# A sum-of-reciprocals kernel: one written-out list of operations replaced by another

## The chip, the cores and the metric

The kernel runs on one core of a Trainium2 chip. Its time is the device time of one execution in microseconds, measured with the profiler off; the median of three such runs of the kernel before is 168.22 us (168.21 to 168.27). A separate profiled execution gives the trace; all durations and moments below come from it, and moments are counted from the start of its span. Engines are written as the profile does: PE is the matrix engine, DVE the vector engine, ACT the scalar (activation) engine, POOL the GpSimd engine and SP the engine that issues the transfers.

## The reference: what is computed

```python
# x: float32, 32 x 512 x 1024, all positive
def reference(x):
    return np.sum(1.0 / x, axis=-1).astype(np.float32)
```

The input has 16384 vectors of 1024 numbers, 67.1 MB; each vector gives one number. Nothing is reused, so every byte is loaded once and used once.

The kernel doesn't divide. It takes the two halves a and b of a vector (512 numbers each) and uses 1/a + 1/b = (a + b) / (a b). The reciprocal of the product a b is made as exp(-ln(a b)) on ACT, with a scale S = 2^17 inside the logarithm that is multiplied out again at the end. One logarithm and one exponential serve two numbers in this way.

## The kernel before: rows, ring, banks and a list of operations

The 16384 vectors lie as 128 partitions by 128 "rows": row r is one vector on each partition, 512 KB in all. The last two rows are each loaded and worked on as two half rows, so that the numbering goes from row 0 to row 129: 0 to 125 are whole, 126 to 129 are halves of 256 KB. Rows live in three places:

- `ring`, 40 row slots in SBUF; row r takes slot r mod 40, so the transfer of row r can't be issued until everything that reads row r - 40 out of the ring is done;
- `prod`, 22 slots in SBUF for products, in which ACT also works;
- `ps`, 8 banks of PSUM.

The order of all work is a list of words, `PLAN`, written out in full and read by a loop at the end of the function. A word is a letter, a row, a count (`+2`) and a bank or product slot (`@6`):

| word | engine, line | what it does |
|---|---|---|
| `Dn` | SP, L187 | load the next n rows (split where the ring wraps round) |
| `Pr+n` | POOL, L199 | product a b of n rows, into `prod` |
| `Cr@b` | PE, L209 | copy the second half of row r to bank b (multiply by the identity) |
| `Vr` | DVE, L220 | product of row r from the ring and the copy in PSUM |
| `Wr` | DVE, L220 | product of row r, both halves from SBUF |
| `Lr+n@p` | ACT, L242 | logarithm of n products, in place, slots p on |
| `Er+n` or `Er+n@b` | ACT, L251 | exponential: in place, or into banks b on |
| `Sr@b` | PE, L232 | a + b of row r into bank b (two multiplications by the identity, accumulated) |
| `Rr` | DVE, L267 | multiply and sum up: the row's result |

A row's product is made in one of three ways (P, V or W). Its last step has two forms. Where the list has an S, R takes the 512 sums in PSUM times the 512 reciprocals in `prod`. Where the E went to PSUM, R takes the whole row of 1024 from the ring times the reciprocals in PSUM, each used twice; the first form costs PE time, the second DVE time.

Each engine does its own words in the order of the list. Between engines, an operation waits for what it reads, and for the last reader or writer of the ring slot, product slot or bank that it overwrites; `note` records this from the order of the list. SP is in order too: a transfer that waits for a ring slot holds back all transfers behind it. When rows 0 to 113 have their results, six small transfers write these out (L289); a last one (L291) writes the rest after the last R.

The lines that issue the loads and those that make the two forms of R are

```python
                    m = min(n, R - a, LAST - r) if r < LAST else 1
                    inst = nc.sync.dma_start(
                        out=ring[:, a : a + m, at : at + 2 * w],
...
                if r in halves:
                    row = prod[:, p, :w]
                else:
                    row = ring[:, q % R, at : at + 2 * w]
```

Of the kernel before, what the change touches and what calls it, by code (L numbers as in the profile page):

```python
# [11 lines left out]
def kernel(  # L12
# [23 lines left out]


    PLAN = """
        D2 D10 D14 D14 P0+2 C3@3 S2@0 V3 P2 L0+2@0 C11@3 S3@1 E0+2@6 P4+2 V11 L2+2@2 R0 S6@2
        E2+2 R1 P6+2 L4+2@4 R2 R3 E4+2@6 S7@0 P8+2 L6+2@8 R4 S10@1 E6+2 R5 P10 L8+2@10 R6 R7  # L40
        S11@2 E8+2@6 L10+2@6 R8 E10+2 R9 D11 R10 R11 P12+2 C19@3 S14@0 V19 P14+2 L12+2@12
        S15@1 E12+2@6 S18@2 R12 P16+2 L14+2@16 R13 E14+2 R14 P18 L16+2@18 R15 S19@0 E16+2@6
        P20+2 L18+2@14 R16 S22@1 E18+2 R17 D9 P22+2 L20+2@20 R18 R19 E20+2@6 S23@2 P24+2
        L22+2@0 R20 E22+2 R21 L24+2@2 R22 R23 E24+2@6 P26 C27@3 R24 S26@0 P28+2 V27 R25 D7
        L26+2@4 C35@3 E26+2 S27@1 P30+2 V35 L28+2@8 R26 S30@2 R27 E28+2@6 P32+2 L30+2@10 R28
        S31@0 E30+2 R29 P34 L32+2@12 S34@1 R30 R31 E32+2@6 P36+2 S35@0 L34+2@6 R32 E34+2 R33
        D7 P38+2 S38@2 L36+2@16 R34 R35 E36+2@6 S39@1 P40+2 L38+2@18 R36 C43@3 E38+2 R37 D6
        S42@0 P42 L40+2@14 V43 R38 E40+2@6 P44+2 R39 S43@2 L42+2@20 R40 E42+2 S46@1 R41 D3
        P46+2 L44+2@0 R42 R43 E44+2@6 S47@0 P48+2 L46+2@2 R44 S50@2 E46+2 R45 P50 L48+2@4
        R46 C51@3 R47 E48+2@6 S51@1 P52+2 V51 R48 D6 L50+2@8 C59@3 E50+2 R49 P54+2 S54@0  # L50
        L52+2@10 V59 R50 E52+2@6 R51 S55@2 P56+2 L54+2@12 R52 E54+2 S58@1 R53 D5 P58
        L56+2@16 R54 R55 E56+2@6 S59@0 P60+2 L58+2@6 R56 S62@2 E58+2 R57 D4 P62+2 L60+2@14
        R58 R59 E60+2@6 S63@1 P64+2 L62+2@18 R60 S66@0 E62+2 R61 D4 P66 L64+2@20 R62 C67@3
        R63 E64+2@6 P68+2 S67@2 V67 R64 L66+2@0 S70@1 R65 D4 E66+2 P70+2 L68+2@2 R66 R67
        S71@0 E68+2@6 P72+2 L70+2@4 R68 D3 E70+2 R69 D2 C75@3 P74 L72+2@10 S74@2 R70 V75
        P76+2 E72+2@6 R71 S75@1 L74+2@8 R72 D2 E74+2 R73 D2 P80 S78@0 L76+2@12 R74 P81
        L80@16 R75 S79@2 E76+2@6 P78+2 L81@17 R76 D2 S81@1 E80@5 E81 R80 L78+2@6 W82 E78+2
        R81 R77 D1 D1 D1 D1 D1 P88 C85@6 S85@1 R78 P83 L88@18 V85 E88@7 R79 P84 S84@0
        L82+2@14 R88 E82+2@5 P86+2 L84+2@19 R82 D1 E84+2 R83 D1 D1 D1 C90@7 P91 L86+2@0
        S91@2 R85 P93 V90 E86+2@5 R84 P92 S90@1 L90+2@2 R87 L93@21 W89 L92@10 R86 D1 D1 D1  # L60
        D1 E93@7 P94 S97@0 E92@6 R93 E90+2 P97 S94@3 L89@11 R92 E89@7 P95 L97@8 R91 S95@4
        E97 R90 L94+2@4 W96 R97 P101 C99@6 L96@9 R89 E94+2 S100@0 P98 V99 E96@5 L101@12 R95
        P100 S99@1 L98@13 R96 E101@7 L99+2@16 R101 E98@6 P104 C103@5 R94 E99+2 S105@2 R98
        P102 L104@18 V103 E104@7 W105 L102+2@6 R100 P107+2 C106@6 L105@14 R104 E102+2@4
        S108@0 V106 E105 R102 L106+3@19 P109 S107@3 R103 P110 E106+3 R105 S106@4 R99 P111+2
        L109+2@0 R107 S112@1 R108 E109+2@6 R106 L111+2@10 P114 R109 S111@0 E111+2 R110 P113
        L114@15 R111 C115@7 P116 L113@2 R112 E114@6 V115 E113@5 S117@0 P117 R114 L116@3
        L115@8 P118 E116@7 R113 S118@1 E115@6 P119 L117+2@12 R116 E117+2 R115 P120 S120@2
        L119@9 R117 P121 L120@4 S121@3 R118 E119@7 E120 R119 P122 L121@5 S122@0 E121 R120
        P123 L122@18 R121 E122 W124 L123@6 R122 L124@7 W125 S125@1 E123@7 E124@6 R123 P126  # L70
        L125@14 P127 L126@16 S127@0 R124 E125 P128 L127@17 S128@2 E126@7 P129 R125 E127
        S129@3 L128@19 R126 L129@20 E128 R127 E129 R128 R129
    """.split()

    Ln = mybir.ActivationFunctionType.Ln
# [246 lines left out]
```

## Time and profile before

| | |
|---|---|
| median of three runs | 168.22 us |
| profiled execution: span from first to last instruction | 166.3 us |
| what lies around the span, by the median | 1.9 us |
| busy: PE, ACT, DVE, POOL | 132.5, 132.3, 128.3, 128.2 us |
| loaded | 67.11 MB, 404 GB/s over the span |
| first product (POOL), second (POOL) | 5.66 us, 17.75 us |
| last DVE instruction ends | 164.0 us |

The page gives no other total for the profiled execution than its span; the 1.9 us around it is the median less the span, and sums below are made against the span and carried over with it. The four engines have nearly the same busy time, some 80% of the span, and the transfer engines are busy almost from end to end. For such a kernel the busy shares say little: what counts is which of five nearly equal streams of work is late at which place, so the profile is read by its chain of waits and by the moments at which rows land.

### The profile page before, as it was taken

Reading aid. Unit: us, or ns where it says so; the run is one execution under the profiler, and the core shown is the slowest. Engines: PE = TensorE matmul, PEld = TensorE weight load, DVE = VectorE, ACT = ScalarE, POOL = GpSimd, SP = SyncE. Lnnn points to the kernel's source line nnn. Section 1 sums busy time; section 2 is a strip of 40 time slices with the busy share of each in tenths; the row PEclk is TensorE's granted clock in tenths of the full one; section 3 lists DMA queues with packets and bytes.
Section 4 is the critical chain, followed back from the end, with each engine's and each line's share of the span. In section 5 each row is a group of like instructions: output and inputs, shape, how many; then the busy total and the mean of one; then the engine's idle time right before and its main releaser. Section 6 shows DMA issues by size and latency. Waiting matters only on the chain.

```text
span 166.3 us, 1348 instructions
## 1 busy us (share of the span) xinstructions
PE 132.5 (80%) x292; PEld 55.2 (33%) x292; DVE 128.3 (77%) x282; ACT 132.3 (80%) x157; POOL 128.2 (77%) x81
## 2 busy tenths in 40 slices
PE   0000799978855999999999999988699979989982
PEld 0000333333312444444343433324234424433351
DVE  0000119885787699898998898989899999999994
ACT  3040073949995899999799999996999999999992
POOL 1500795069995999999999999948977869999860
PEclk9999999999996999999999999999999999999999
DMA  5999999999998989999999999999999999999940
GB/s 189 536 394 394 441 441 441 441 441 441 441 441 349 509 368 446 430 417 438 441 434 434 406 426 446 429 424 424 414 437 437 414 410 428 410 409 410 400 139 4
DMA packets 5768, 67.26 MB, mean 404 GB/s; under 512 B 1536, under 2 KB 1536, under 8 KB 3200
## 3 DMA queue, kind: packets, MB, share of 16 engines
q1 hardware_dynamic: 5760, 67.18, 95.6%
q8 instruction: 2, 0.03, 0.1%
q14 instruction: 6, 0.05, 0.1%
HBM read 67.11 MB, written 0.07 MB: 404 GB/s over the span
## 4 chain that ended last, share of the span: by engine, by line
DMA 57%; PE 18%; ACT 8%; DVE 6%; POOL 6%; issue 3%; SPq 1%; ACTq 0%; POOLq 0%; DVEq 0%
DMA ring<-in_x_dram 57%; PE ps L232 15%; POOL prod L199 6%; ACT prod L242 4%; PE ps L209 3%; ACT ps L251 2%; DVE ring L267 2%; DVE prod L267 2%; ACT prod L251 2%; DVE prod L220 1%; SPq L187 1%; DVE sums L267 0%; ACTq L242 0%; POOLq L199 0%; DVEq L317 0%
## 5 line engine op out<-in xcount | busy, mean ns | idle before, releaser
L199 POOL TENSOR_TENSOR prod<-ring 128x1024 f32<-128x1024 f32 (+2 forms) x75 | 127.5, 1727 | 33.5 <-DMA ring<-in_x_dram 27.1
L232 PE MATMUL ps<-ring,ident 128*128 128x512 f32 (+1 forms) x260 | 116.9, 596 | 5.2 <-DVE sums L267 4.5
L242 ACT ACTIVATE prod<-prod 128x1024 f32<-128x1024 f32 (+2 forms) x78 | 68.5, 892 | 24.9 <-DVE prod L220 14.3
L267 DVE CUSTOM_DVE_ANT_1 ring<-ring,ps 128x1024 f32<-128x1024 f32 (+1 forms) x65 | 76.4, 1208 | 8.9 <-ACT ps L251 8.7
L232 PEld LDWEIGHTS ps<-ring,ident 128*128 128x128 f32 x260 | 49.2, 193 | 71.7 <-issue 51.6
L267 DVE CUSTOM_DVE_ANT_0 prod<-prod,ps 128x512 f32<-128x512 f32 (+1 forms) x63 | 40.9, 677 | 0.4 <-PE ps L232 0.4
L209 PE MATMUL ps<-ring,ident 128*128 128x512 f32 x32 | 19.3, 689 | 25.7 <-DMA ring<-in_x_dram 24.0
L251 ACT ACTIVATE ps<-prod 128x1024 f32<-128x1024 f32 (+2 forms) x41 | 34.1, 838 | 4.5 <-DVE sums L267 3.7
L251 ACT ACTIVATE prod<-prod 128x1024 f32<-128x1024 f32 (+3 forms) x37 | 34.4, 931 | 0.9
L220 DVE TENSOR_TENSOR prod<-ring,ps 128x512 f32<-128x512 f32 x16 | 10.9, 684 | 26.3 <-PE ps L209 26.3
L209 PEld LDWEIGHTS ps<-ring,ident 128*128 128x128 f32 x32 | 6.0, 213 | 36.0 <-issue 21.4
L267 DVE DVE_READ_ACCUMULATOR2_ANT sums<- 128x1 f32 x130 | 10.7, 82 | 0.0
L220 DVE TENSOR_TENSOR prod<-ring 128x512 f32<-128x512 f32 x6 | 4.1, 688 | 0.1
L84 ACT ACT_TABLE_LOAD x1 | 1.3, 1283 | 0.7 <-PEq L306 0.7
L267 DVE CUSTOM_DVE_ANT_0 prod<-prod,ps,sums 128x256 f32<-128x256 f32 x2 | 0.9, 475 | 0.0
masks.py:197 POOL MEMSET ident<- 128x128 f32 x1 | 0.2, 204 | 0.3 <-POOLq L306 0.3
masks.py:199 POOL TENSOR_SCALAR_AFFINE_SELECT ident<-ident 128x128 f32<-128x128 f32 x1 | 0.3, 292 | 0.1
L306 POOL MEMSET const-float32-0.0<- 128x1 f32 x1 | 0.1, 98 | 0.2 <-issue 0.2
L306 POOL MEMSET const-bfloat16-1.0<- 128x1 bf16 x1 | 0.1, 101 | 0.0
L306 POOL MEMSET const-uint8-127<- 128x1 uint8 x1 | 0.1, 101 | 0.0
L306 POOL MEMSET const-float32-1.0<- 128x1 f32 x1 | 0.1, 98 | 0.0
## 6 DMA issues: line engine op xcount, KB each, us to landing
ring<-in_x_dram SPq DMA_DIRECT2D x2, 7168.0 KB, 41.2
ring<-in_x_dram SPq DMA_DIRECT2D x2, 3584.0 KB, 29.3
ring<-in_x_dram SPq DMA_DIRECT2D x2, 3072.0 KB, 31.9
ring<-in_x_dram SPq DMA_DIRECT2D x3, 2048.0 KB, 34.0
ring<-in_x_dram SPq DMA_DIRECT2D x1, 5632.0 KB, 30.3
ring<-in_x_dram SPq DMA_DIRECT2D x5, 1024.0 KB, 31.8
ring<-in_x_dram SPq DMA_DIRECT2D x1, 5120.0 KB, 16.5
ring<-in_x_dram SPq DMA_DIRECT2D x1, 4608.0 KB, 30.7
```

The costliest lines, as they stand in the source:

```text
L84: nc.scalar.add_instruction(mybir.InstLoadActFuncSet(name=nc.get_next_instruction_name(), act_func_set_id=act_sets.index("natural_log_exp_ ...
L187: inst = nc.sync.dma_start(out=ring[:, a : a + m, at : at + 2 * w], in_=x_v[:, q : q + m, at : at + 2 * w],)
L199: inst = nc.gpsimd.tensor_tensor(out=prod[:, p : p + m, :w], in0=ring[:, a : a + m, at : at + w], in1=ring[:, a : a + m, at + w : at + 2 * w],
L209: inst = nc.tensor.matmul(ps[:, b, : place(r)[2]], lhsT=ident, rhs=xs(r, 1), start=True, stop=True,)
L220: inst = nc.vector.tensor_tensor(out=prod[:, p, :w], in0=xs(r, 0), in1=in1, op=mult)
L232: inst = nc.tensor.matmul(ps[:, b, : place(r)[2]], lhsT=ident, rhs=xs(r, h), start=h == 0, stop=h == 1,)
L242: inst = nc.scalar.activation(out=pg, in_=pg, func=Ln, scale=S)
L251: inst = nc.scalar.activation(out=rc, in_=pg, func=Exp, scale=-1.0)
L267: inst = nc.vector.tensor_tensor_reduce(out=row, in0=row, in1=other, scale=S, scalar=total if q in summed else 0.0, op0=mult, op1=add, acc ...
L306: nc = _bacc.Bacc("TRN2", target_bir_lowering=False, num_devices=1)
```

## The change

Only the text of `PLAN` differs; the loop, the buffers and the lines after it are the same, six lines further down (L232 is L238, L242 is L248 and so on). Counted by words:

| | before | after |
|---|---|---|
| transfers of rows | 33 | 32 |
| first transfers, rows | 2, 10, 14, 14, 11, 9, 7, 7 | 15, 14, 11, 8, 10, 8, 8, 6 |
| P of one row, of two | 38, 33 | 72, 14 |
| C and V (product through PSUM) | 16 | 23 |
| W (product from SBUF) | 6 | 3 |
| L of one row, of two, of three | 23, 50, 1 | 66, 27, 2 |
| E of one row, of two, of three | 23, 50, 1 | 112, 7, 0 |
| S of whole rows | 62 | 60 |
| R over a whole row of 1024 | 64 | 66 |
| R over 512 sums | 62 | 60 |

The half rows 126 to 129 are left out of the lower eight lines; each has 4 P, 4 L, 4 E, 3 S and 4 R of half size in both lists. The ring's wrap splits the words D19 and D11 of the new list into 11 and 8 and into 6 and 5 rows.

Before, an `L` of two rows is mostly followed at once by the `E` of the same two rows, in row order. After, rows are taken out of order within about ten rows, and between the `L` and the `E` of a row there are mostly other words. The diff, cut to the beginning, the parts that are spoken of below, and the end:

```diff
     PLAN = """
-        D2 D10 D14 D14 P0+2 C3@3 S2@0 V3 P2 L0+2@0 C11@3 S3@1 E0+2@6 P4+2 V11 L2+2@2 R0 S6@2
-        E2+2 R1 P6+2 L4+2@4 R2 R3 E4+2@6 S7@0 P8+2 L6+2@8 R4 S10@1 E6+2 R5 P10 L8+2@10 R6 R7
...
-        P123 L122@18 R121 E122 W124 L123@6 R122 L124@7 W125 S125@1 E123@7 E124@6 R123 P126
-        L125@14 P127 L126@16 S127@0 R124 E125 P128 L127@17 S128@2 E126@7 P129 R125 E127
-        S129@3 L128@19 R126 L129@20 E128 R127 E129 R128 R129
+        D15 P2 P0 C1@0 C4@1 V1 P3 L0+3@0 V4 L3+2@3 E4@2 R4 E3 E2@3 C7@4 R2 P11 E1@5
+        P10 P13 D14 S3@6 L10+2@5 E11@7 P5+2 C8@0 V8 P9 R1 L5+2@9 S0@1 L8@11 V7 E6
+        L7@13 E7@2 P14 E5@3 R11 L13+2@7 S6@0 S8@5 E0 R3 R7 E14 C12@4 S14@7 P18 V12 R5
+        D19 L12@15 C28@6 P17 P15 C16@2 E13@4 P21 L18@14 E8 R0 R14 R13 S19@3 V28 V16
...
+        R21 R32 S24@3 E38 E29@7 E35 R31 L39@12 S35@0 E37@4 R34 R22 C44@1 D8 P40 P41
+        R35 R38 L42+2@6 L46+2@14 E39@2 P56 E42+2 P57 R37 V44 S47@6 S43@0 L40@20 R39
+        S42@5 P53 P54 P51 C48@4 E47 E46@1 R43 R29 E33@2 L44+2@3 R24 E36@0 L41@18 R46
+        P52 R36 E41@7 R47 E45@3 P50 C55@1 R42 R41 L56@13 V48 E40 L48@21 P49 E44@0 R33
+        E56@6 S51@5 P58+2 S55@7 V55 E48@4 S40@2 P62+2 L53+2@0 R44 R48 L57@19 D8 E54@1
...
+        E114+2 R113 P122 E116@4 R111 L117@8 R115 L118@6 R114 E117 L119@9 E118@1 R116
+        L120@12 P123 E119 S122@3 S123@2 E120@5 L121@17 E121 R117 R118 L122@11 R119
+        P126 R120 P127 E122 R121 P128 P129 W124 L123@10 R122 W125 L124@13 E123 E124@4
+        S125@0 R123 L125@14 L126@0 E125 E126@1 R124 R125 L127@7 L128@4 E127 S127@7
+        R126 S128@5 S129@6 L129@3 R127 E128 E129 R128 R129
     """.split()
```

## The prediction

> **What bounds the kernel now.** I read the page first (busy shares, the 40 slices), then the end of the chain of waits, then the timelines of the opening and of the last 8 us, then the groups with shapes kept apart.
>
> ```profile
> PE 132.5 (80%) x292; PEld 55.2 (33%) x292; DVE 128.3 (77%) x282; ACT 132.3 (80%) x157; POOL 128.2 (77%) x81
> ...
> DMA  5999999999998989999999999999999999999940
> ...
> HBM read 67.11 MB, written 0.07 MB: 404 GB/s over the span
> ```
>
> No engine is full; the transfer engines are, from slice 2 to slice 38. The end of the chain shows how the stream and the end hang together:
>
> ```profile
> 147.18 10.17 DMA ring<-in_x_dram
> 157.34 0.02 issue
> ...
> 158.81 1.72 PE ps L232 x4
> ...
> 163.54 0.08 DVE sums L267
> 163.63 0.39 DVE prod L267
> ```
>
> The chain rides on the transfers until row 124 lands. The trace's landing records (one per transfer engine) have row 125 complete at 158.7, and in the timeline PE begins then and stops no more:
>
> ```profile
> 158.81 4.54 PE L232 MATMUL ps<-ring,ident 128*128 128x512 f32 x16 [1.12 <-DVE sums L267]
> ...
> 163.54 0.47 DVE L267 CUSTOM_DVE_ANT_0 prod<-prod,ps,sums 128x256 f32<-128x256 f32 x1
> ```
>
> Those 16 matmuls are S125, S127, S128 and S129: the fixed tail. Row 125 lands, 0.1, 4.54 on PE to 163.35, then R129 to 164.0; 5.3 us in all. (The wait is put down to DVE; the landing falls in the same 0.1 us.) So the bound is the stream of transfers up to row 125 plus 5.3 us. The median is 168.22, the span 166.3; the 1.9 between them is carried over.
>
> The opening shows when work can start:
>
> ```profile
> 5.66 2.34 POOL L199 TENSOR_TENSOR prod<-ring 128x1024 f32<-128x1024 f32 x1 [4.36 <-DMA ring<-in_x_dram]
> ...
> 17.75 8.20 POOL L199 TENSOR_TENSOR prod<-ring 128x512 f32<-128x512 f32 x4 [9.75 <-DMA ring<-in_x_dram]
> ...
> 17.81 2.04 PE L209 MATMUL ps<-ring,ident 128*128 128x512 f32 x2 [17.81 <-DMA ring<-in_x_dram]
> ```
>
> Each engine starts when a whole transfer has landed: two rows at 5.66, ten more at 17.75, 1.21 us per row.
>
> **The change, part by part.**
>
> *The stream.* The same 67.1 MB. The last 21 pieces (4, 4, 4, 3, 2, 2, 2, 2 rows, nine single rows, four halves) are alike in both lists, and in all there are 32 pieces for 33. A row costs 1.21 us in pieces of 14 (17.75 to 34.69) and 1.28 us as a single row (landings of 117 to 125: 148.5 to 158.7), so 0.07 us per piece: -0.1 us. Each piece must be issued before the queue runs dry. From issue (0.74) to landing (5.66) D2 took 4.9 us, of which 2.5 are its two rows, so the lead has to be 2.4 us.
>
> *The opening.* The first piece has 15 rows and lands at 17.75 + 3 x 1.21 = 21.4. What goes is the early start of POOL and ACT on two rows (2.34, and 1.06 + 1.03) and 3.7 us of everything else: between 0 (hidden) and 3.7 + 2.1 = 5.8 us on ACT. I take 0 for the time, because work left over is done while the stream, which doesn't wait for it, goes on until 158.7; the cover is the free time worked out below, and if it is gone the cost is one to one. PE's slow start (first matmuls 0.85 to 0.9 us, later 0.43) comes 3.6 us later too and is paid inside the 4.0 us that PE waits for rows 15 to 28.
>
> *Work per engine.* Steps from start to start, from rows in which an engine ran without a wait: POOL 2.34 for two rows, 1.25 for one; DVE 1.14 (whole row), 0.61 (sums), 0.60 (product); PE 0.43 a matmul; ACT 0.96 for two rows, 0.52 for one, and 0.13 more when an E follows at once on its own L (1.09 between such starts, 0.96 otherwise).
>
> ```profile
> 88.01 1.05 ACT L242 ACTIVATE prod<-prod 128x1024 f32<-128x1024 f32 x1
> 89.09 1.06 ACT L251 ACTIVATE prod<-prod 128x1024 f32<-128x1024 f32 x1
> 90.05 1.04 ACT L242 ACTIVATE prod<-prod 128x1024 f32<-128x1024 f32 x1
> ```
>
> - ACT: 66 more instructions. 100 two-row and 46 one-row become 34 and 178 (and two triples of 1.4 for two): 63.4 less, 68.6 more, +5.3. But E right behind its own L falls from 52 cases to 18: -4.4. Sum 132.0 to 132.8.
> - POOL: 19 doubles fewer (-44.5), 34 singles more (+42.5): 127.5 to 125.6.
> - DVE: 2 more whole-row R (+2.3), 2 fewer of the other (-1.2), 7 V more and 3 W fewer (+2.4): 125.8 to 129.3.
> - PE: 7 C more (14 matmuls, +6.0), 2 S fewer (8, -3.4): 123.1 to 125.7.
>
> The sums of before agree with its busy times to 2% except PE's, whose records overlap and include slow starts.
>
> The Trainium skill, ScalarE: Activation LUTs, section What ACT_TABLE_LOAD costs, speaks against splitting: every ACTIVATE has 186 ns of fixed cost, of which back-to-back ones overlap 93. By that rule 66 more would be an estimated +6.1 us on ACT and a list near 138 us, which would end ACT past the stream. The trace agrees on the step (0.52 against 0.48 per row) but shows what the rule doesn't have: the overlap is lost when E reads what the L before it wrote.
>
> *Does it fit in?* I ran the sums forward in list order: P, C, S and W not before their row lands (the landings of before by rows loaded), L not before its product, R not before its E and S. For before this gives DVE's end 164.1 (the trace: 164.0). For after: L0+3 needs V1, P2 and P0 (two POOL steps: 23.9), and from there to the same last E at 163.3 ACT has 139.4 us for 132.8 of work, 6.6 free. It must wait for late rows at L5 (1.2), L18 (1.6), L58 (0.6), L61 (1.1) and some small ones, 5 in all, the last big one at 92. About 1.6 us of slack remain from there to the end; POOL keeps 0.7 behind P86; DVE and PE over 2.5. The end comes out at 163.7 by DVE (R123 is now 0.61 in place of 1.14), but S129 still ends at 163.35, and R129 needs 0.05 + 0.47 + 0.08 after it: 163.9, so -0.1.
>
> *Waits on banks and slots.* Compared pair by pair in those sums, a producer comes later than its consumer wants it at six places in after (S6 on V8 1.6, S8 on R1 1.0, C44 on R31 0.5, S47 on R22 1.4, S51 on R42 0.5, L48 on V48 1.6) and at seven in before (up to 2.5). All six lie before 78 us. Behind S6 on PE stand C12 and C28, but C28 waits 4.0 for its row; behind S47 stands C48, which waits 4.0; behind L48 stand all later L and E, and L58 and L61 then wait 1.6 less. I take 0 in sum; between 0 and 1.6.
>
> *SP.* D19's second half needs R5 (37.2 by the sums, queue dry at 52), D10 needs S9 (48.6; 62), D8 R22 (66.7; 75), the second D8 R33 (79.5; 84.4), all later ones have 11 us or more. The tightest lead is 4.9 us against the 2.4 needed: 2.5 us of room. Before, by the same sums, leads were 20 us or more. D5 waits for the late S85 (131, needed at 157).
>
> Sum: -0.1 (tail and pieces overlap there) = 163.9 for DVE's end, 168.1 us.
>
> **The rivals.**
>
> *ACT or POOL end behind the stream (slower).* For it: from L61 on ACT has no free time, and in before ACT fell behind its own forward sum by 1.06 us within 55 us (L78+2 at 110.69 against 109.6). At that rate 65 us cost 1.25, inside the 1.6; at twice the rate 2.5, so +0.9; with the 1.6 of L48 unhidden on top +2.5. POOL's 0.7 is thinner still. Against it: the list leaves its E and R more time behind their producers than before (E behind P is over 2 us in 40 cases, 3 before). It decides once 1.6 us are lost on ACT after 92: 169.0 to 170.6.
>
> *The stream runs dry at the second D8 (slower).* If R33 is more than 2.5 us late against 79.5, each further us goes straight to the end; L48's 1.6 us wait is near it. Against: R33's E stands before L48. With 2 us over: 170.1.
>
> *The stream gets faster (faster).* Of the 16 transfer engines the first is done with D2 0.4 us before the last, with row 125 2.0 us: the last ones are held up singly, at moments that coincide with small transfers on the two instruction queues (2 and 6 packets on the page). Another list shifts these. Between +0.8 and -1.6 us; half of the gain, -0.8: 167.4.
>
> *The change does nothing for the time because the opening is hidden* is the forecast; its opposite, the opening in full, would be 168.2 + 5.8 = 174, and no cover speaks for it.
>
> **How the numbers follow.** 0.2% of 168.2 is 0.34 us, about what a measurement can tell. The stream and fixed tail as now: 0.57, 168.1, with 0.35 inside 0.34 us and the rest split by the instruction queues, 0.10 faster and 0.12 slower. ACT or POOL late: 0.25, slower. Stream dry: 0.08, slower. Stream faster: 0.10. Faster 0.20, same 0.35, slower 0.45. The range takes the half gain below and ACT's rival above: 167.4 to 170.4; the likeliest case alone is 167.6 to 168.7.
>
> **What would show it.** Right: first product at 21.4, POOL's wait for P18 ending near 38.3, row 125 landing at 158 to 159.5, PE without a gap from there, ACT's sum of busy time near 133 to 140 (records overlap). Wrong: row 125 landed and S125 waiting over 0.5 us for a bank; L123 waiting for nothing with rows long landed; slices of DMA share under 8 near 84 us; row 125 outside 158 to 159.5.

## The result and the profile after

The changed kernel takes 169.08 us (median of five executions, 168.71 to 170.1), the kernel before 168.27 beside it (168.21 to 168.4): a ratio of 1.0055, with a 95% interval of 1.003 to 1.008. It is 0.8 us slower. The forecast was 168.1 us, no change. Ratios are of fast executions alone: of the old list with the big opening, further down, four of twelve executions took 171.1 to 171.7 us and count as slow.

The page of the changed kernel. Its profiled execution is one of the quicker ones, 168.89 us with a span of 167.1.

```profile
PE 132.3 (79%) x298; PEld 56.3 (34%) x298; DVE 131.5 (79%) x286; ACT 134.7 (81%) x223; POOL 126.2 (76%) x96
...
PEclk9999999999999999996999999999999999999999
DMA  7999999999799999999999999999999999999940
```

The busy times of POOL and DVE moved as the sums had them: -2.0 and +3.2 for -1.9 and +3.5. ACT's rose by 2.4 where the sum had 0.8; its records overlap, so that its busy time is not the sum of its steps. (PE's can't be compared: its records lengthen with the granted clock, the row PEclk.) The transfer engines are as full as before. Nothing on this page says where 0.8 us went.

The timeline of the opening: the first product starts at 21.8, not at 21.4.

```profile
21.81 9.75 POOL L205 TENSOR_TENSOR prod<-ring 128x512 f32<-128x512 f32 x7 [20.50 <-DMA ring<-in_x_dram]
```

The chain of waits, in order of time (start, us, what):

```profile
79.27 1.13 DVE ring L273
80.40 0.02 DVE sums L273
...
80.44 0.33 SPq L193
...
80.81 21.14 DMA ring<-in_x_dram
...
110.45 29.75 DMA ring<-in_x_dram
...
140.27 2.47 POOL prod L205 x2
...
153.21 1.30 POOL prod L205
...
154.53 0.03 ACT prod L248
...
163.53 0.32 ACT prod L257
...
163.87 0.15 DVE prod L273
...
164.35 0.39 DVE prod L273
```

The DVE result at 80.40 is R33, and what SP issues at 80.44 is the second D8 (rows 66 to 73), with the next piece right behind it. (The chain of before has a result on DVE ahead of an issue too, at 101.9 us.)

The end differs as well. Before, the chain goes with the transfers up to row 124, as shown above. Here it leaves them at 140.2 and goes over POOL, which works from P109 on almost without a gap, and from 154.53 over ACT, which has waited for P120 and has no gap from L120 to E129. R128 waits for E128 (over at 163.83), and R129 follows R128. PE is through with S129 at 163.91. In the kernel before it was DVE that had no gap from W125, at 158.69, to the end; PE was through at 163.35, and R129 began at 163.54, right behind R128. Two windows of before show it:

```profile
core 0: us, PE busy (x) PEld busy (x) DVE busy (x) ACT busy (x) POOL busy (x), PEclk, DMA share, GB/s
160.00:162.00 2.00, 2.00 (x9) 1.43 (x8) 2.00 (x5) 2.00 (x7) 2.00 (x4) 1.00 0.20 36
162.00:164.00 2.00, 1.35 (x7) 0.85 (x5) 2.00 (x10) 1.30 (x5) 0.23 (x1) 1.00 0.02 4
```

The trace has 16 landing records for each transfer, one per transfer engine. From them:

| | before | after |
|---|---|---|
| first piece complete | 5.59 (2 rows) | 21.74 (15 rows) |
| row 125, mean of the 16 engines | 157.18 | 157.92 |
| row 125, complete (last engine) | 158.67 | 159.20 |
| last DVE instruction ends | 164.03 | 164.76 |
| from row 125 to that end ("tail") | 5.36 | 5.56 |

So 0.5 us come with the stream and 0.2 behind it. The theories to be told apart were: the second D8 is issued too late (the rival with a chance of 0.08); the bigger opening; and ACT or POOL being behind the stream (the rival with 0.25).

### The profile page after: what moved, and what is told of

Read it like the earlier page. It is cut to its first block, busy times and chain, and to the rows that moved or that the text cites. A ratio compares the mean times of both kernels' runs of the same rounds, so it can differ in the third digit from the quotient of the medians.

```text
span 167.1 us, 1420 instructions
## 1 busy us (share of the span) xinstructions
PE 132.3 (79%) x298; PEld 56.3 (34%) x298; DVE 131.5 (79%) x286; ACT 134.7 (81%) x223; POOL 126.2 (76%) x96
## 4 chain that ended last, share of the span: by engine, by line
DMA 53%; POOL 20%; DVE 11%; ACT 6%; issue 3%; PE 3%; another core or an unknown queue 1%; SPq 1%; DVEq 0%
DMA ring<-in_x_dram 53%; POOL prod L205 20%; DVE ring L273 6%; ACT prod L248 3%; DVE prod L273 3%; ACT prod L257 2%; PE ps L238 2%; ACT ps L257 1%; PE ps L215 1%; DVE prod L226 1%; SPq L193 1%; DVE sums L273 0%; DVEq L323 0%
## 5 line engine op out<-in xcount | busy, mean ns | idle before, releaser
L205 POOL TENSOR_TENSOR prod<-ring 128x512 f32<-128x512 f32 (+2 forms) x90 | 125.5, 1432 | 36.0 <-DMA ring<-in_x_dram 35.6
L238 PE MATMUL ps<-ring,ident 128*128 128x512 f32 (+1 forms) x252 | 111.1, 589 | 2.5 <-DVE sums L273 1.7
L248 ACT ACTIVATE prod<-prod 128x512 f32<-128x512 f32 (+3 forms) x99 | 71.0, 742 | 28.1 <-DVE prod L226 24.8
L273 DVE CUSTOM_DVE_ANT_1 ring<-ring,ps 128x1024 f32<-128x1024 f32 (+1 forms) x67 | 79.6, 1209 | 3.5 <-ACT ps L257 3.3
L238 PEld LDWEIGHTS ps<-ring,ident 128*128 128x128 f32 x252 | 47.7, 192 | 64.1 <-issue 50.9
L215 PE MATMUL ps<-ring,ident 128*128 128x512 f32 x46 | 25.6, 660 | 29.1 <-DMA ring<-in_x_dram 28.7
L257 ACT ACTIVATE ps<-prod 128x512 f32<-128x512 f32 (+2 forms) x63 | 37.7, 608 | 0.4
L226 DVE TENSOR_TENSOR prod<-ring,ps 128x512 f32<-128x512 f32 x23 | 15.7, 685 | 27.0 <-PE ps L215 26.8
L257 ACT ACTIVATE prod<-prod 128x512 f32<-128x512 f32 (+2 forms) x60 | 36.7, 626 | 0.2
L215 PEld LDWEIGHTS ps<-ring,ident 128*128 128x128 f32 x46 | 8.7, 204 | 43.1 <-issue 28.7
L226 DVE TENSOR_TENSOR prod<-ring 128x512 f32<-128x512 f32 x3 | 2.1, 689 | 0.7 <-DMA ring<-in_x_dram 0.7
```

Source lines behind the costliest of these rows:

```text
L205: inst = nc.gpsimd.tensor_tensor(out=prod[:, p : p + m, :w], in0=ring[:, a : a + m, at : at + w], in1=ring[:, a : a + m, at + w : at + 2 * w],
L215: inst = nc.tensor.matmul(ps[:, b, : place(r)[2]], lhsT=ident, rhs=xs(r, 1), start=True, stop=True,)
L226: inst = nc.vector.tensor_tensor(out=prod[:, p, :w], in0=xs(r, 0), in1=in1, op=mult)
L238: inst = nc.tensor.matmul(ps[:, b, : place(r)[2]], lhsT=ident, rhs=xs(r, h), start=h == 0, stop=h == 1,)
L248: inst = nc.scalar.activation(out=pg, in_=pg, func=Ln, scale=S)
L257: inst = nc.scalar.activation(out=rc, in_=pg, func=Exp, scale=-1.0)
```

## Experiments: the opening

First the changed kernel once more.

> The changed kernel once more, unedited, for a second trace beside the kernel before. Two theories are open for the 0.8 us. STREAM: row 125 lands later (159.2 against 158.7 in the first two traces) because the transfers lose time at three places: the first piece of 15 rows (complete 0.4 us later than 17.75 + 3 x 1.21), and the second D8, whose issue waits for R33 until 80.4 us, so that three transfer engines start its first packet 0.8 to 1.0 us late at 83 us. ENGINES: the late start (21.8 us) used up the engines' free time, so that ACT is behind at the end and R128 and R129 wait for E128 and E129 (tail of 5.55 us in place of 5.35). Both expect 169.1 again. STREAM expects row 125 complete at 159.0 to 159.4 and the late first packets at 83 us again; ENGINES expects a tail of 5.5 us or more again. If row 125 comes at 158.7 and the time is still 169, STREAM falls.

It took 169.09 us (168.59 to 169.61), ratio 1.0047 (1.0031 to 1.0064). The eleven executions of the changed kernel spread over 1.5 us, the 22 of before beside them over 0.6.

Then the opening alone, put into the list of before, and the other way round.

```diff
 before_big_open (list of before)
-D2 D10 D14 D14 P0+2
+D15 D14 D11 P0+2
 after_small_open (new list)
-D15 P2 P0
+D2 D10 D3 P2 P0
```

> The kernel before with only its opening replaced: D2 D10 D14 D14 becomes D15 D14 D11, the pieces of the changed list, all else as before. STREAM (first piece): row 125 complete 0.3 to 0.4 us later, 168.6. ENGINES: the list of before had 2 to 3 us of slack behind 90 us, so the 4 us later start costs 0 to 1.5: 168.3 to 169.8, with the tail longer than 5.35. If the opening is hidden here and the pieces cost nothing: 168.3.

> The changed list with only its first word replaced: D15 becomes D2 D10 D3, so that 12 rows have landed by 17.8 us and not 21.8, and nothing else moves. STREAM (first piece): row 125 complete 0.3 to 0.4 us earlier, 158.8, time 168.6. ENGINES: 4 us more free time for ACT and POOL, the tail back to 5.3 us, 168.8 to 168.9, and less scatter between runs than 168.7 to 170.1. Both at once: 168.4. If neither holds: 169.1.

The big opening costs the old list 0.2 us: 168.5, ratio 1.0011 (1.0001 to 1.002). All engines start 4 us later than with 12 rows, and this is hidden. Row 125 is complete at 158.93, 0.26 later than before, and the tail is 5.40. The small opening makes the new list worse: 169.78 (168.81 to 171.05), ratio 1.0088 (1.0057 to 1.0119). The tail stays at 5.55, so the opening has nothing to do with it. What is worse is the stream: in the trace, taken in the slowest of the six executions, R33 ends at 81.63, 1.2 us later than with the big opening, and row 125 is complete at 161.36 (mean of the engines 158.46; one engine is 2.2 us behind all others). Why R33 is late came out only later (the section on the clock).

## Experiments: when the second D8 is issued

Four edits move the moment at which rows 66 to 73 are issued and leave the work as it is. Rows 66 to 72 need results up to R32, which are early; only row 73 needs R33.

```diff
 after_d8_early
-R43 R29 E33@2 ... L57@19 D8 E54@1 ... R53 D11 E55
+R43 R29 D7 E33@2 ... L57@19 D7 E54@1 ... R53 D5 E55
 after_r33_early
-L41@18 R46 ... E44@0 R33 E56@6
+L41@18 R33 R46 ... E44@0 E56@6
 after_d8_split71
-R43 R29 E33@2 ... L57@19 D8 E54@1
+R43 R29 D7 E33@2 ... L57@19 D1 E54@1
 after_r33_late
-E44@0 R33 E56@6 ... V55 E48@4 S40@2 P62+2 L53+2@0 R44
+E44@0 E56@6 ... V55 R44 R33 E48@4 S40@2 P62+2 L53+2@0
```

> The changed list with the second D8 D11 cut differently into the same number of pieces: rows 66 to 72 are issued after R29 (about 8 us earlier in the list than R33), then rows 73 to 79, then 80 to 84. STREAM (late issue): no late first packets near 83 us, row 125 complete 0.2 to 0.3 us earlier, 168.8. ENGINES: no change, 169.1. If the late packets go and the time stays, the late issue was on transfer engines that were ahead anyway.

> The changed list with one word moved: R33, which releases the ring slot that the second D8 (rows 66 to 73) waits for, goes five DVE operations forward, ahead of R46. Pieces and work are the same. STREAM (late issue): R33 ends at 76 to 77 us in place of 80.4 and D8 is issued then; no first packets 0.6 to 1.3 us late at 82 to 84 us; row 125 complete 0.3 to 0.5 us earlier (158.8 to 158.9, as with before_big_open), time 168.6. ENGINES: the tail stays 5.5 us; if lateness of the engines were the cause, 169.1 unchanged.

> The changed list with the second D8 cut into D7 (rows 66 to 72, issued after R29) and D1 (row 73, issued where the D8 was). Unlike after_d8_early, row 73 lands with its neighbours, at about 95 us and not at 101.9. STREAM (late issue): the queue always has the 7 rows, so no late packets at 83; one piece more costs 0.07; row 125 at 158.9, time 168.7. The 5 us of after_d8_early were the wait of C73 (5.4 us on PE) and all behind it: they must be gone here. If 173 to 174 comes again, that reading is wrong and the early issue itself does harm.

> The dose in the other direction: in the changed list R33 is moved back behind V55 and R44, two DVE operations of 0.6 and 1.14 us, so that it ends at about 82.1 us in place of 80.4 and the second D8 is issued then, while the transfers before it are done on the fastest engine at 83.0. STREAM (late issue; 2.4 us from issue to data): D8's first packets come at about 84.6, some 1.6 us after the queue is dry, against 0 to 0.5 before; row 125 at 160.3 to 160.8, time 170.0 to 170.6. If the stream were only held up by engines' traffic at that time and not by the issue: 169.1.

The issues of SP in the timeline, first of the changed kernel, then with R33 early, then with R33 late (start, us of the group of issues, engine, line):

```profile
80.44 0.80 SPq L193 DMA_DIRECT2D ring<-in_x_dram  x2
```

```profile
75.17 2.61 SPq L190 DMA_DIRECT2D ring<-in_x_dram  x2
```

```profile
82.77 0.80 SPq L190 DMA_DIRECT2D ring<-in_x_dram  x2
```

| | median (range), us | issue of rows 66 to 73 | lateness of their first packets, mean of 16 engines | row 125, mean |
|---|---|---|---|---|
| changed kernel | 169.08 (168.71 to 170.1) | 80.44 | 0.2 | 157.92 |
| R33 early | 168.75 (168.62 to 168.85) | 75.17 | 0 | 157.57 |
| 7 + 1 rows | 168.66 (168.58 to 168.83) | 73.50, row 73 at 80.49 | 0 | 157.77 |
| R33 late | 170.78 (170.34 to 171.03) | 82.77 | 0.7, and a late start | 159.32 |

A piece of 8 rows moves in packets of 32 KB, one per partition, eight per transfer engine. "Lateness" is what the first ones took over their usual 1.21 us. In the changed kernel three of the sixteen took 2.0 to 2.2 us, with R33 late all sixteen 1.7 to 2.1. It differs between executions: in the changed kernel's second trace, with the issue at 80.44 again, fourteen packets took 1.5 to 2.5 us, and the mean of row 125 is 158.20. The page's row of slices is too coarse for this, and in a window of 2 us only the loss with R33 late shows. These are the windows from 82 to 84 us, columns as in the section on the result, first of the changed kernel, then with R33 late:

```profile
82.00:84.00 2.00, 2.00 (x6) 0.85 (x5) 1.81 (x5) 2.00 (x5) 2.00 (x2) 1.00 1.01 393
```

```profile
82.00:84.00 2.00, 1.57 (x4) 0.68 (x4) 2.00 (x5) 2.00 (x5) 2.00 (x2) 1.00 0.69 213
```

With R33 late, R33 ends 2.3 us later than in the changed kernel (82.73 for 80.40), and the time is 1.7 us longer, 2.0 longer than with R33 early. The first transfer engine was through with the rows before at 82.82, the engines' mean at 83.43; the issue at 82.77 plus the 2.4 us from issue to data is 85.2, so 1.7 to 2.3 us too late. Beyond the room, the price is about one to one. R33 early takes 0.33 off (ratio to before 1.0028, 1.0018 to 1.0038), the split 0.42 (1.0023, 1.0013 to 1.0033), and with both the spread shrinks to about 0.25 us. Only two of the eleven executions of the changed kernel are as quick as the slowest of these seventeen. So the late issue costs 0.35 to 0.4 us at the median and up to a microsecond more in single executions. In the profiled execution with R33 early the gain stands in the mean of the engines (157.57 against 157.92) and not in the last one (159.18 against 159.20); the time gained rests on the medians.

Loading early but in other pieces was the costly miss: 173.91, ratio 1.0351 (1.032 to 1.0381), with row 125 complete at 158.89. Row 73 had gone from a piece that lands at 94.7 into one that lands at 101.9, and C73 stands on PE before everything else. The waits of this run from 88 to 104 us (us in total, times, longest), and PE's timeline:

```profile
PE ps L212 <- DMA ring<-in_x_dram: 5.4, 1, 5.4
```

```profile
94.69 1.88 PE L235 MATMUL ps<-ring,ident 128*128 128x512 f32 x4
102.02 2.05 PE L212 MATMUL ps<-ring,ident 128*128 128x512 f32 x2 [5.45 <-DMA ring<-in_x_dram]
```

The tail became 10.8. Towards the end of the wait of 5.4 us PE's granted clock fell to 0.5, from 99.7 to 106.5, as in the section on the clock below; what the wait and what the clock cost was not told apart. The page's row:

```profile
PEclk9999999999999999987999956999999999999999
```

From there on the engines had no room to give it back.

## Experiments: is ACT or POOL behind the stream?

Eight logarithms between rows 91 and 104 are not issued, 4.2 us of ACT:

```diff
-L91@13 ... L94@15 ... L97@14 ... L95@6 ... L96@9 ... L98@17 ... L99@10 ... L104@0
```

> The changed list with the logarithms of eight single rows (91, 94 to 99 without 100, and 104) left out, so that ACT has 4.2 us less to do from about 118 us on; those rows' results are not the reference's. ENGINES: ACT is no longer behind the stream, E123 follows row 123 sooner and the tail goes from 5.55 to 5.35 or less; if lateness of ACT were the whole loss, 168.3. STREAM: row 125 stays at 159.2 to 159.4, time 168.8 to 169.1.

169.26 (168.72 to 169.28), ratio 1.0048 (1.0035 to 1.0061), tail 5.56: no change. ACT's own work is not what holds this list back: here too ACT stands until P120 ends (154.62) and takes L120 at 154.65.

## Experiments: the small opening, and PE's clock

With R33 early, the small opening was tried again; then with useless work for PE in its two gaps (a word K, a C whose result nobody reads); then with two pieces; then K with the big opening.

```diff
 after_r33_early_small_open (R33 early)
-D15 P2 P0
+D2 D10 D3 P2 P0
 after_r33_early_small_open_warm (that, and)
-L12@15 C28@6 ... P51 C48@4
+L12@15 K14@6 K14@6 K14@6 K14@6 K14@6 K14@6 C28@6 ... P51 K47@4 K47@4 C48@4
 after_r33_early_d2d13 (R33 early)
-D15 P2 P0
+D2 D13 P2 P0
 after_r33_early_warm (R33 early, D15 as it is)
-P51 C48@4
+P51 K47@4 K47@4 C48@4
```

> R33 forward and the opening D2 D10 D3 together. STREAM: both losses of the transfers are gone, row 125 as in the kernel before (158.7), and the time is 158.7 + 5.5 + what lies around: 168.3 to 168.5. ENGINES: with 4 us more free time the tail is back at 5.3 as well: 168.2. If the small opening does harm of its own (it gave 169.8 alone, with R33 at 81.6), 169 or more.

> after_r33_early_small_open (170.99) with eight useless matmul pairs added on PE: six of row 14 into bank 6 ahead of C28 (where PE stood idle for 5.8 us until 38.6) and two of row 47 into bank 4 ahead of C48 (75 us). CLOCK: the granted clock stays 1.0 at 35 to 42 us, PE isn't behind, the tail falls from 10.1 to 5.5 us, time 168.3 to 168.6. ORDER (the early start itself disturbs the sequence of waits): 170.5 to 171.5 as before; extra work on PE can only harm.

> R33 forward as in after_r33_early (168.75), and D15 cut into D2 and D13. Rows 0 and 1 land at 5.7, but POOL's first product is row 2, so that the engines still start at 21.5 and PE isn't left idle in mid-work. STREAM (first piece: 15 rows complete at 21.7 to 22.0 in place of 21.4): 0.2 us earlier throughout, row 125 at 158.9, time 168.5 to 168.6. If the first piece is not it: 168.8 (one piece more).

> after_r33_early (168.75) with two useless matmul pairs ahead of C48, where PE waited 2.3 us and the clock was 0.5 to 0.7 at 76 to 80 us. CLOCK: the drop goes; since this list's end is held by the transfers, the time stays 168.6 to 168.75, with row 125 and the tail as they are. If the remaining tail of 5.54 is an effect of the drop: tail 5.36, 168.5.

The small opening with R33 early took 170.99 (170.67 to 173.03) instead of 168.75. Row 125 was complete at 158.84, early, but the tail was 10.1. The cause stands at 31 to 42 us. Its PE timeline, its windows, and its page's row of the granted clock:

```profile
30.97 1.88 PE L235 MATMUL ps<-ring,ident 128*128 128x512 f32 x4
38.64 3.62 PE L212 MATMUL ps<-ring,ident 128*128 128x512 f32 x4 [5.78 <-DMA ring<-in_x_dram]
```

```profile
36.00:38.00 2.00, 0.00 (x0) 0.00 (x0) 0.34 (x2) 0.00 (x0) 0.00 (x0) 0.50 0.68 293
38.00:40.00 2.00, 1.36 (x2) 0.84 (x3) 0.00 (x0) 0.13 (x1) 1.43 (x2) 0.50 0.99 428
```

```profile
PEclk9999999965999999697599999999999999999996
```

PE started early, ran out of rows and stood for 5.8 us; then four matmuls took 3.6 us, and the clock fell again later. (With R33 where it was, the small opening has the same stop, and 0.5 from 35.7 to 42.5; that R33 is late there for this reason was not tested by itself.) With the gap filled, the same place and the same row:

```profile
32.88 5.31 PE L222 MATMUL ps<-ring,ident 128*128 128x512 f32 x12
38.53 1.98 PE L213 MATMUL ps<-ring,ident 128*128 128x512 f32 x4 [0.34 <-DMA ring<-in_x_dram]
```

```profile
PEclk9999999999999999999999999999999999999999
```

168.49 (168.33 to 168.66), ratio 1.0014 (1.0005 to 1.0023), with the tail back at 5.55: work that computes nothing took 2.5 us off. This is the best time of the new list with all its work in it, and 0.26 under the same list with the big opening (168.75, with or without the two K47). Two pieces, 2 and 13 rows, leave a gap of 2.1 us at 38 and gave 170.1 (168.65 to 170.89), ratio 1.0105 (1.0066 to 1.0144); execution by execution the time goes roughly with the clock, 168.65 at a mean of 0.99, 169.29 and 169.44 at 0.986, 170.75 to 170.89 at 0.96 to 0.978. With the big opening, the gap before C48 (2.3 us, at 75) is followed by a slow clock too, but filling it changed nothing: 168.75 (168.61 to 169.64), ratio 1.0041 (1.0025 to 1.0057). There the rest of the kernel can take it; with the small opening and R33 early it can't.

## Experiments: the tail

What was left is the tail, 5.53 to 5.56 in every variant in which the clock stayed up and no W was added. A product on POOL was left out, or given to DVE (`W112` for `P112`), in several surroundings:

```diff
 after_r33_early_less_p, after_small_open_warm_less_p
-R100 P112 V103
+R100 V103
 after_small_open_warm_less_2p (that, and)
-R104 P114 D1
+R104 D1
 after_r33_early_warm_w112, after_three, after_three_warm
-R100 P112 V103 ... R102 S114@5
+R100 V103 ... R102 W112 S114@5
```

(The "three" have R33 early and D2 D13, the second of them two K14 and two K47 as well.)

> R33 forward, and the product of row 112 on POOL left out (row 112's results are not the reference's), so that POOL has 13 and not 14 products to make from row 109 on (14 took 17.94 us, the rows land within 16.4). If the tail of 5.54 us comes from POOL, P123 ends 0.2 us earlier behind its row and the tail is 5.35 to 5.4, time 168.55. If the tail is in the order of the last words themselves: 5.54 and 168.75.

> All three repairs, with the whole computation: R33 forward, D2 D13 for D15, and row 112's product moved from POOL (P112) to DVE (W112, after R102). If the loss is the sum of late issue 0.35, first piece 0.2 and POOL's tail 0.2, then row 125 at 158.9, tail 5.4 and 168.3 to 168.4, the time of the kernel before. If the parts hide each other or W112 delays DVE: 168.6 or more.

> after_three (R33 forward, D2 D13, W112 in place of P112; 170.17) with two useless matmul pairs ahead of C28 and two ahead of C48. CLOCK: no stretch at 0.5 at 38 or 76 us, tail 5.4, row 125 at 158.9, time 168.3 to 168.4. ORDER: 170 as before.

> after_r33_early with the two matmul pairs ahead of C48 and row 112's product on DVE (W112) in place of POOL: the whole computation, big opening kept. If POOL's backlog makes the tail: 5.36 to 5.4, time 168.5. If the tail is in the order of the last words: 5.54, 168.7.

> after_r33_early_small_open_warm (168.49, row 125 at 158.99, tail 5.55) with POOL's product of row 112 left out (row 112's results are not the reference's). If POOL's backlog from row 109 on makes the tail: P123 0.2 us earlier behind its row, tail 5.35 to 5.4, time 168.3. If the tail lies in the order of the last words: 5.55 and 168.5.

> The new list with R33 moved forward, the opening of 2, 10 and 3 rows, the useless matmuls in the two gaps of PE, and two products on POOL left out, those of rows 112 and 114 (these two rows' results are therefore not the reference's; the rest of their work is done on what stands in their product slots). What is open is why the stretch from the landing of row 125 to the last DVE instruction is 5.54 us with this list and 5.36 before. In five traces DVE's end follows the end of POOL's product of row 123 by 6.54 to 6.55 us (before: 164.03 and 157.49; the new list: 164.76 and 158.21; with row 112 left out: 164.32 and 157.77), and that product ends 1.43 us after row 123 has landed before, 1.57 with the new list, 1.55 with row 112 left out. Theory A, POOL's lag: the last ten products follow each other without a gap, one per row that lands, and keep the lag with which they begin, which comes from rows 113 and 114 landing as one piece and being worked on one after the other. Without row 114's product, POOL waits for row 116, the lag is 0.13 there and 0.15 to 0.20 at row 123: its product ends 1.43 to 1.48 after the landing, DVE 6.55 later, and the stretch is 5.40 to 5.46. Theory B, the order of the list's last words on ACT, PE and DVE sets it: the product of row 123 ends earlier, 6.55 becomes 6.65 and the stretch stays at 5.53 to 5.55. By A the time is 0.1 us under the kernel with row 112 alone left out (168.4 against 168.5), by B the same.

| | median (range), us | tail | P123 ends after row 123 landed |
|---|---|---|---|
| before | 168.27 (168.21 to 168.4) | 5.36 | 1.44 |
| old list, big opening | 168.5 | 5.40 | 1.43 |
| changed kernel | 169.08 (168.71 to 170.1) | 5.56 | 1.57 |
| R33 early, less P112 | 168.65 | 6.64 | 1.51 |
| R33 early, W112 | 169.46 (169.32 to 169.67) | 6.31 | 1.54 |
| three | 170.17 (169.36 to 170.94) | 6.47 | 1.57 |
| three, K | 169.23 (169.19 to 169.49) | 6.35 | 1.56 |
| small opening, K, less P112 | 168.53 (168.37 to 168.91) | 5.53 | 1.55 |
| that, less P114 | 168.48 (168.25 to 168.63) | 5.54 | 1.54 |

Leaving out one product changed nothing, and leaving out a second right before the last ten rows changed nothing either, although POOL then waited 1.15 us for row 116. So no backlog that POOL brings to row 116 makes the tail longer, and the theory that POOL keeps a lag it brought along fell. (The 6.64 is an execution at a mean clock of 0.98; this kernel's times were 168.48 to 168.81 at 0.99 and above, and 169.81 and 170.05 at 0.98.) Giving the product to DVE cost 0.7 us (169.46 against 168.75), and the three repairs together, expected at 168.3 to 168.4, took 170.17, with K 169.23.

The run with two products left out shows what else happens on POOL. Its timeline where POOL begins row 116, right after a wait:

```profile
147.36 0.69 DVE L233 TENSOR_TENSOR prod<-ring 128x512 f32<-128x512 f32 x1 [0.33 <-DMA ring<-in_x_dram]
...
147.40 1.79 POOL L203 TENSOR_TENSOR prod<-ring 128x512 f32<-128x512 f32 x1 [1.15 <-DMA ring<-in_x_dram]
```

P116 takes 1.79 us, and beside it runs W115, DVE's product with both halves from SBUF. The changed kernel has the same pair at the same place, in the timelines of DVE and of POOL:

```profile
147.71 0.69 DVE L226 TENSOR_TENSOR prod<-ring 128x512 f32<-128x512 f32 x1 [0.71 <-DMA ring<-in_x_dram]
...
147.80 1.74 POOL L205 TENSOR_TENSOR prod<-ring 128x512 f32<-128x512 f32 x1
```

Over all traces of this case, 1308 one-row products on POOL with no W beside them took 1.25 to 1.32 us. Those that began with 0.48 to 0.65 us of a W still to run took 1.62 to 1.79, the overlap less 0.14 more than the usual 1.28; one that began 0.17 before a W's end took 1.31. Where the W comes second, it is DVE's that is long: W115 took 1.64 and 1.78 us where it began 0.18 and 0.03 us into a product. In the run with W112 it begins in the middle of one product (1.05 us instead of 0.69) and holds up the next:

```profile
148.57 1.05 DVE L232 TENSOR_TENSOR prod<-ring 128x512 f32<-128x512 f32 x1
...
149.06 1.71 POOL L202 TENSOR_TENSOR prod<-ring 128x512 f32<-128x512 f32 x1
```

In the kernel before, four of the six W stand where POOL is idle anyway; of the last two, W124 meets the end of a product for 0.13 us and W125 meets none. As an example, W89:

```profile
122.79 0.69 DVE L220 TENSOR_TENSOR prod<-ring 128x512 f32<-128x512 f32 x1
...
123.81 3.76 POOL L199 TENSOR_TENSOR prod<-ring 128x512 f32<-128x512 f32 x3 [1.14 <-DMA ring<-in_x_dram]
```

The Trainium skill, SBUF — State Buffer, section SBUF: two separate sides, has the rule: a DVE operation with two inputs from SBUF and a POOL operation that reads SBUF lock each other out for a whole instruction, whichever comes second. The records agree but for the 0.14 us, with 0.46 us lost by P116.

How this reaches the end stands in the chain of waits above. P116 starts 0.12 us after its row landed, P117 0.54. A product takes 1.24 from start to start and a row lands every 1.28, so the products behind it stay late: P120 starts 0.41 after its row and ends at 154.50. ACT has stood for 0.12 us by then, takes L120 at 154.53 and has no gap from there on. In 16 of the 18 traces of the new list DVE ends 10.21 to 10.24 us after L120 begins. P123 is not waited for: it ends at 158.21, and L123 starts at 158.47, behind E122. (That DVE ends 6.53 to 6.56 us after P123 in both lists comes from two different chains.)

With P116 at its usual 1.28 us, L120 could begin 0.33 earlier, right behind E118, and 0.2 to 0.3 us of it would reach the end (L124 needs W124, which is over 0.2 before L124 begins). That is all of the 0.2 by which the tail is longer. That P116 lost 0.46 us to W115 is measured; that this makes the tail longer is worked out. Moving W115 elsewhere was not tried.

## Why the prediction was wrong

**The step that failed** is the one on SP: "The tightest lead is 4.9 us against the 2.4 needed: 2.5 us of room." The mechanism, the place (the second D8 behind R33) and the price (each further us straight to the end) were those of the rival with a chance of 0.08; the room was mis-sized twice. R33 ended at 80.40 where the forward sum had 79.5: 0.9 less. (In the trace DVE has no gap from R31, which waits for E31 until 64.6, to R33; PE waited 1.3 us for its row at C28 and 2.3 at C48, where the sums had 4.0 each. The engines were behind the sums by then.) And "queue dry 84.4" is when the last transfer engines are through with rows 58 to 65 (84.94 in the trace). The first was through at 83.01, and a transfer engine that is through early doesn't wait for the others. From the issue at 80.44 to 83.01 it is 2.6 us against 2.4 needed: 0.2 us of room, and by the times of the single executions mostly less than none. Cost: 0.35 to 0.4 us.

**The stream, "-0.1"**, left out the first piece. 15 rows were complete at 21.7 to 22.0, not 21.4: the first transfer engine was through at 21.0, but the slowest sets the moment. The big opening alone cost 0.2 us in the old list and 0.26 in the new one (168.75 against 168.49), near the limit of what can be told. The traces agree: with R33 early, row 125 is complete at 158.8 to 159.0 where the first piece has two rows, and at 159.0 to 159.2 where it has 15. How the two pieces' start costs this much was not taken further.

**The fixed tail, "-0.1"**, came out at +0.2. The prediction took it to be PE's 4.5 us, and by PE it would have been 5.3 (S129 is over at 163.91, and R129 needs 0.6). It set the W at nothing but their time on DVE ("7 V more and 3 W fewer"). What W115 does to POOL was in neither the sums nor the rivals. The end moved to ACT, which waits for POOL's P120.

The three together, 0.35 to 0.4 and 0.2 and 0.2, are the 0.8 measured; the first two rest on runs, the cause of the third is worked out.

**Right:** the opening's later start is hidden (the old list with it: 168.5); the busy times of POOL and DVE moved as summed; row 125 landed between 158 and 159.5, and from then on PE had no gap (S125 to S129, 159.44 to 163.91). **ACT's rival** (0.25) fell as far as ACT's own work goes: 4.2 us less of it changed nothing. Its POOL half came true in a small way, by the 0.2 us of the tail. It was right that slack is thin: a wait of 5.4 us on PE at 97, and the slow clock that came with it, made the tail 5.2 us longer. And the sign given for a dry stream, "slices of DMA share under 8 near 84", can't show this case: a slice is 4.2 us, and the hole is 0.2 us per engine.

No version of the new list beat the kernel before. The repaired one (R33 early, small opening, filled gap) stands at 168.49, 0.14% above it.

## What to carry to other kernels

Measure the room of a transfer from the engine that runs dry first, not from the landing of the piece, and take a forward sum's own error off it: here 2.5 us of room were 0.2. When a list moves an operation between engines, look at what runs beside it at the new place: a product on DVE with both inputs in SBUF cost the one on POOL 0.46 us. Work that starts earlier can be worse if it then runs out of input: PE's clock pays for the gap.

## What the runs showed of the hardware

PE's granted clock fell to 0.5 for 3.41 us or 6.83 us at a time. Each trace can be cut into stretches of 3.41 us, counted from the start of its first record at full clock. In the twenty traces, up to PE's last matmul, fifteen stretches at full clock in which PE stood for 2.06 to 3.12 us in all were followed by one at 0.5, and so was one with 1.77; three with 1.85 to 1.92 were not, nor was any other with less. So a stop of 2.4 us that lay across two stretches (eight logarithms left out, at 73.0) left the clock alone, and one of 2.1 us within one (2 and 13 rows, at 36.3) did not. The Trainium skill, TensorE: Matmul & The Clock Gate, section What's actually happening, tells of such a gate with a free-running window of about 3.4 us, and of half the clock after an idle window; here 60% of a window was enough. Useless matmuls in the gap took 170.99 to 168.49.

The sixteen transfer engines take their queue at their own pace. From first to last they were 0.3 to 0.6 us apart at the end of a first piece of two rows, 0.7 to 1.0 with 15 rows, and 1.8 to 2.5 at row 125 (3.6 in one trace). In the first trace of the changed kernel a piece issued at 80.44 had its first packets stretched from 1.21 to 2.0 to 2.2 us on three engines only, and with the issue 2.3 us later on all sixteen.
